# Four more pairs of FFN blocks in seven half-size products, with a load list of their own for the weight parts

## The chip, the core and the metric

The kernel runs on one core of one Trainium2 chip, as one program. The metric is device time in microseconds (us), median of three runs. TensorE (PE) multiplies, VectorE (DVE) and ScalarE (ACT) work on tiles, GpSimd (POOL) does small work and issues a few transfers, and SyncE (SP) issues nearly all of them. Each engine takes its instructions in the order of its own program and waits for semaphores of the others.

## The reference, cut to what matters

A two-layer decoder trunk on 256 tokens of width 1024, in float32, with four SwiGLU FFNs of hidden width 2816:

```python
def swiglu(h, w_gate, w_up, w_down):
    return (jax.nn.silu(h @ w_gate) * (h @ w_up)) @ w_down

for layer in range(2):
    x = x + 0.5 * swiglu(rms_norm(x, ffn1_norm[layer]), ...)
    h = rms_norm(x, mix_norm[layer])
    mem_n = rms_norm(mem, mem_norm[layer])
    x = x + (mlstm_mixer(h, mem_n, ...) if layer == 0 else dilated_mixer(h, mem_n, k_sh, v_sh, ...))
    x = x + 0.5 * swiglu(rms_norm(x, ffn2_norm[layer]), ...)
    if layer == 0:
        kv = rms_norm(x, kv_norm) @ w_kv      # shared keys (QK-normed) and values, used by layer 1
```

The dilated mixer adds a bias by distance to its scores; both mixers also attend to the 256 memory tokens.

## The kernel before, in words

**One product in three passes.** Operands are float32; each is split into a high part (a rounded copy, ScalarE) and a low part (the rest, VectorE), and a product is the sum of three passes, low by high, high by high and high by low (`mm3`, L773). Most passes are 128x512: 128 rows of the contraction, 512 columns of weights.

**Weight units.** Weights come in units of 128x1024 (512 KB) in the order in which PE uses them (`_stream`, L100). A unit is loaded by SP into one of six `raw` tiles, split by ScalarE (`hi`, 1024 columns) and VectorE (`lo`), and stands in a ring of eight `hi`/`lo` pairs until PE has used it (`emit_unit`, L631). So the two engines can be at most eight units ahead of PE.

**An FFN.** Its width is cut into eleven blocks of 256 (`FB`). `g b` multiplies both halves of the tokens (t = 0, 1) with gate and up of block b: four units, 2 x 8 x 3 = 48 products, into PSUM banks named `gups`. ScalarE makes the silu (`sil`), VectorE the hidden block `h`, which goes to DRAM and back turned (`hb`, `hd`, `ht`; `placed`, L1036), and is split (`hhb`, `hlb`). `d b` multiplies it with the down weights: two units, 24 products into `acc`. A plan orders the `g`, `d` and other steps (`_plan`, L81); the order of the instructions on each engine is then set by a planner in the kernel that carries its own estimate of each engine's clock (`_Model`, L241 on) and emits what is ready first.

**Pairs in seven products.** Two FFNs, named (layer, which) = (0,2) and (1,2), take blocks 5 and 6 together. The contraction is cut in two and the two blocks' weights and the two halves of x are combined so that seven products of half length stand for eight (a form of Strassen's method). Step `mb` of a plan is product m of the pair that begins with block b, so `25` is product 2 of the pair (5, 6). Each is 4 row chunks x 3 passes = 12 products on PE from two units, so a pair takes 84 in place of 96. What it needs beside:
- Sums and differences of x, once per FFN (`sums`, L1102; tiles `xs`, `xd`, `th`, `tl`).
- Three kinds of weight parts in two row groups (k = 0, 2): slot a (`pa`), b (`pb`) and c (`pc`), loaded by SP, some with a second part added on top by a transfer from POOL (`next_part`, L584), and remade by VectorE between the products (`remade`, L609): a-b after product 5, then b+a after 3, c-a after 4; b also takes another part by an adding transfer from POOL. `SLOTS` says which product uses which slot; every one of the fourteen units is split as usual.
- Combinations of the seven results (`seventh`, L1130): `e` is a copy of product 2, then `g` is product 5 plus `e`; products 4, 3 and 7 go on adding to the PSUM banks of 2, 5 and 1, so 4 waits for the copy, 3 for the first `g`, and 7 for the third `g`, the one that reads product 1. VectorE makes five more such sums (`c21`, `c12`, `f`, `c22`, `c11`), and four hidden blocks come out.

The order in which the products come is 2, 5, 4, 3, 1, 6, 7 in all plans.

**When parts are loaded.** Parts stand in the same list as the other units; one pair is open at a time (`self.open`), and while other units are loaded every third of them pulls one part from `todo` (`early`, L595, `EVERY = 3`), at most fourteen units early.

**The attention of layer 1.** After FFN (0,2), `shared_kv` (L1662) makes keys (`kTs`), values (`vs`) and the bias, which lies as a table of differences in DRAM (`diag`) and is read into a tile `bias`. All three stay in SBUF through FFN (1,1) until `mixer_b` (L1716). The eight chunks of mixer B's output weights are split in advance during (0,2) and (1,1), in steps called `pre` (`AHEAD_OF`), stored as `wo` in DRAM and reloaded in mixer B.

Of the kernel before, what the change touches and what calls it, by code (L numbers as in the profile page):

```python
# [48 lines left out]
AHEAD_OF = {(0, 2): (9,), (1, 1): (2, 3, 4, 5, 6, 7, 8)}  # L49

PLANS = {(1, 2): "g0 g1 g2 d0 g3 d1 g4 d2 25 55 45 35 d3 15 65 d4 75 g7 g8 d5 d6 g9 d7", (0, 2): "g0 g1 g2 d0 g3 d1 g4 25 55 d2 45 35 d3 15 65 d4 75 g7 g8 d5 d6 g9 d7"}
# [6 lines left out]
EVERY = 3  # L61
# [3 lines left out]

SLOTS = {2: ("a", (0,), None), 5: ("b", (3,), None), 4: ("c", (2, 0), None),
# [14 lines left out]
def _plan(layer, which):  # L81
# [4 lines left out]
    for what, b in ((s[0], int(s[1:])) for s in PLANS.get((layer, which), default).split()):  # L86
# [8 lines left out]
        if what == "d" and b + 2 in AHEAD_OF.get((layer, which), ()):  # L95
            plan.append(("pre",))
# [144 lines left out]
class _Model:  # L241
# [71 lines left out]
    def product(self, columns, cycles, rows, outs, ins):  # L313
# [9 lines left out]
        self.run("tensor", cycles / (2400 if self.fast else 1200) + 0.0027, outs, ins)  # L323

    def run(self, engine, cost, outs, ins, delay=0.0):
# [8 lines left out]
        for a in outs:  # L334
            self.mark(a, end, True, engine)
        self.latest = max(self.latest, end)


class _Engine:
# [5 lines left out]
    def __getattr__(self, method):  # L345
        call, model, name = getattr(self.engine, method), self.model, self.name

        def traced(out, *args, **kw):
# [8 lines left out]
            if name == "sync" or name == "gpsimd" and method == "dma_start":  # L357
                model.run("sync", max(n * out.partition_size() * 4 / 360e3, 0.06), outs, ins, 2.0)
# [51 lines left out]
class _Kernel:  # L410
    def __init__(self, tc, ctx, io, out, units):
# [18 lines left out]
        self.stored, self.slots, self.made, self.open, self.partp = {}, {}, {}, None, None  # L430
        self.todo, self.turn = [], 0
# [123 lines left out]
    def load_unit(self):  # L555
        i, self.loaded = self.loaded, self.loaded + 1
        if self.units[i][1] is None:
            return
        width = self.units[i][2]
        if self.units[i][1][0] == "parts":  # L560
            self.load_part(i)
            return
# [7 lines left out]
    def load_part(self, i):  # L570
        key = self.units[i][0]
        if self.open != key[1:4]:
            self.begin_parts(key[1:4])
        slot = SLOTS[key[4]][0], key[5]
        while slot not in self.slots:
            self.next_part()
        self.raw[i] = self.slots[slot]

    def begin_parts(self, pair):
        self.open = pair  # L580
        self.slots = {}
        self.todo = [(m, k) for m, k in ((4, 0), (2, 0), (4, 2), (2, 2), (5, 0), (5, 2))]

    def next_part(self):  # L584

        m, k = self.todo.pop(0)
        slot, parts, _ = SLOTS[m]
        t = self.work.tile([P, 1024], F32, tag="mem", name="pa") if slot == "a" else \
            self.partp[1].tile([P, 1024], F32, tag=f"p{slot}{k}", name=f"p{slot}{k}")
        self.slots[slot, k] = t  # L590
        self.nc.sync.dma_start(t, self.part_of(self.open + (parts[0], k)))
        for p in parts[1:]:
            self.nc.gpsimd.dma_start(t, self.part_of(self.open + (p, k)), accum_op=ALU.add)

    def early(self):  # L595

        for i in range(self.loaded, min(self.next + EARLIER, len(self.units))):
            key, src = self.units[i][:2]
            if src and src[0] == "parts" and self.open is None and self.may_load(i):
                self.begin_parts(key[1:4])  # L600
        self.turn += 1
        if self.todo and (self.todo[0][0] != 5 or self.summed) and self.turn % EVERY == 0:
            self.next_part()
# [5 lines left out]
    def remade(self, pair, m, k):  # L609

        nc = self.nc
        a, b, c = (self.slots.get((n, k)) for n in "abc")
# [9 lines left out]
        elif m == 7 and k == 2:  # L622
            self.open = None
# [7 lines left out]
    def emit_unit(self):  # L631
# [48 lines left out]
        while self.loaded <= i:  # L680
            self.room()
            self.load_unit()
        if src is None:
# [12 lines left out]
    def loads(self):  # L696

        while self.loaded < len(self.units) and self.loading() < RAW and \
                (self.units[self.loaded][1] is not None or self.loaded == self.next) and \
                self.may_load(self.loaded):  # L700
            self.load_unit()
            self.early()
# [4 lines left out]
    def may_load(self, i):  # L707

        key, src = self.units[i][:2]
        return src is None or src[0] != "parts" or \  # L710
            self.open in (None, key[1:4]) and self.partp is not None and \
            self.partp[0] == key[1:3] and (key[4] != 5 or self.summed)

    def room(self):
        while self.loading() >= RAW:
            self.finish(self.running[0])
        key, src = self.units[self.loaded][:2]
        if not self.may_load(self.loaded):
            self.finish(self.made[self.open, 7, 2])

    def unit_ready(self):
# [8 lines left out]
        if i not in self.raw:  # L730
            return 1e9
        key = self.units[i][0]
# [4 lines left out]
        at = max(model.ready(self.raw[i][:, :self.units[i][2]]),  # L737
# [248 lines left out]
    def ffn(self, layer, which, after, memory=None):  # L986
        with ExitStack() as ctx:
            self.partp = None
            self.ffn_in(layer, which, after, memory, self.pool(ctx, f"ffn{layer}{which}"))

    def ffn_in(self, layer, which, after, memory, fp):
# [6 lines left out]
        pairs = (layer, which) in PLANS  # L998

# [11 lines left out]
        def hidden(b, t):  # L1011
            def steps(ps):
# [6 lines left out]
                hh = self.work.tile([P, FB], F32R, tag="hh", bufs=5, name="hh")  # L1019
                hl = self.work.tile([P, FB], F32R, tag="hl", bufs=5, name="hl")  # L1020
# [15 lines left out]
        def placed(b, before):  # L1036
# [7 lines left out]
            yield  # L1044
            hh = fp.tile([P, 4, 4, 32], F32R, tag="hh", bufs=4, name="hhb")
# [22 lines left out]
        def dn(b, t):  # L1068
# [5 lines left out]
            parts = hT.pop((b, t))  # L1074
# [901 lines left out]
```

## Time and profile before

| | us |
|---|---|
| runs | 985.94, 984.80, 982.86 |
| median | 984.8 |
| span of the profiled execution | 981.7 |
| median less that span | 3.1 |

The span runs from the first to the last instruction of one profiled execution; the runs' times are of the whole execution. A matmul's time in the trace overlaps the next one's, since they are pipelined, so the cost of one is the distance between starts. In the rows, `out<-in` names tiles by the program's names, `xN` is a count, and what stands in square brackets or behind a bar is the engine's idle time before it and what ended that.

### The profile page before, as it was taken

The page shows a single profiled execution, that of the slowest core. Times are in us where ns is not written, and L with a number is a line of the kernel's source. Part 1 is how long each engine was busy: PE and PEld are TensorE (multiplying, and loading weights), DVE is VectorE, ACT ScalarE, POOL GpSimd, SP SyncE. Part 2 cuts the span into 40 slices and gives each one's busy share as a digit, 9 for nine tenths or more (in the row PEclk, how much of TensorE's full clock was granted, in tenths as well). Part 3 has the DMA queues.
Part 4 walks back from the last instruction along what each step waited for, and adds up shares of the span by engine and source line. Part 5 has one row for each costly group of instructions (what it writes and reads, how often), then busy time and mean ns, then how long its engine had stood idle before and what let it go on. Part 6 is the DMA issues. An engine that isn't in the chain of part 4 may idle for free.

```text
span 981.7 us, 13154 instructions
## 1 busy us (share of the span) xinstructions
PE 973.7 (99%) x4655; PEld 809.8 (82%) x4655; DVE 691.0 (70%) x1035; ACT 563.8 (57%) x903; POOL 52.2 (5%) x86
## 2 busy tenths in 40 slices
PE   9999999999999999999999999999999999999998
PEld 6888888899998888888878888888887788878887
DVE  5856656569886787976586677776576679589653
ACT  7656445477565655655466566565564585465541
POOL 0002000010010000000011000000002000000000
PEclk9999999999999999999999999999999999999999
DMA  9968677346355697388657688889627557945751
GB/s 353 321 212 302 212 239 227 112 148 230 118 193 193 202 318 243 116 290 268 235 179 252 226 318 274 336 301 316 246 86 266 207 175 252 375 99 205 272 166 43
DMA packets 85482, 223.95 MB, mean 228 GB/s; under 512 B 8172, under 2 KB 29608, under 8 KB 85416
## 3 DMA queue, kind: packets, MB, share of 16 engines
q1 hardware_dynamic: 84120, 218.88, 64.5%
q0 software_dynamic: 1152, 4.19, 2.3%
q8 instruction: 36, 0.59, 0.3%
q14 instruction: 30, 0.25, 0.1%
q10 hardware_dynamic: 144, 0.04, 0.0%
HBM read 203.66 MB, written 19.42 MB: 227 GB/s over the span
## 4 chain that ended last, share of the span: by engine, by line
PE 95%; DVE 2%; ACT 1%; DMA 1%; issue 1%; SPq 0%; DVEq 0%; ACTq 0%
PE gups L763 47%; PE acc L763 24%; PE aps L763 8%; PE oacc L763 4%; PE kvps L763 3%; PE bqps L763 2%; PE mkvps L763 2%; PE tps L770 1%; DVE s L349 1%; PE po L763 1%; PE tpp L770 1%; PE sc L763 1%; DMA ht<-hd 0%; PE ms L763 0%; PE pn L763 0%
## 5 line engine op out<-in xcount | busy, mean ns | idle before, releaser
L349 DVE TENSOR_TENSOR lo<-raw,hi 128x1024 fp32r<-128x1024 f32 (+2 forms) x263 | 302.7, 1167 | 85.2 <-ACT hi L349 79.7
L349 ACT CAST hi<-raw 128x1024 fp32r<-128x1024 f32 (+2 forms) x263 | 260.1, 1008 | 95.3 <-PE acc L763 40.9
L763 PE MATMUL gups<-lo,xh 128*128 128x512 f32 x656 | 254.9, 391 | 1.6 <-DVE g L349 1.6
L763 PE MATMUL gups<-hi,xh 128*128 128x512 f32 x656 | 254.6, 390 | 0.4 <-ACT hi L349 0.4
L763 PE MATMUL gups<-hi,xl 128*128 128x512 f32 x656 | 254.4, 390 | 0.0
L763 PEld LDWEIGHTS gups<-lo,xh 128*128 128x128 f32 x656 | 123.2, 188 | 27.3 <-DVE g L349 2.1
L763 PEld LDWEIGHTS gups<-hi,xh 128*128 128x128 f32 x656 | 123.3, 188 | 26.4 <-ACT hi L349 1.3
L763 PEld LDWEIGHTS gups<-hi,xl 128*128 128x128 f32 x656 | 123.4, 188 | 26.0
L349 ACT ACTIVATE sil<-gups,rstd 128x256 f32<-128x256 f32 x84 | 39.7, 474 | 146.4 <-PE gups L763 136.3
L763 PE MATMUL acc<-lo,hhb 128*128 128x512 f32 x304 | 119.5, 393 | 0.0
L763 PE MATMUL acc<-hi,hlb 128*128 128x512 f32 x304 | 118.6, 390 | 0.1
L763 PE MATMUL acc<-hi,hhb 128*128 128x512 f32 x304 | 118.3, 389 | 0.0
L349 DVE SCALAR_TENSOR_TENSOR lo<-raw,gains,hi 128x512 fp32r<-128x512 f32 x144 | 99.6, 744 | 16.4 <-ACT hi L349 16.1
L349 DVE SCALAR_TENSOR_TENSOR h<-gups,rstd,sil 128x256 f32<-128x256 f32 x84 | 40.0, 480 | 91.1 <-ACT sil L349 91.0
L349 ACT ACTIVATE hi<-raw,gains 128x512 fp32r<-128x512 f32 x144 | 93.9, 715 | 14.9 <-PE gups L763 5.8
L763 PEld LDWEIGHTS acc<-hi,hlb 128*128 128x128 f32 x304 | 57.1, 188 | 12.4 <-DVE hlb L349 0.5
L763 PEld LDWEIGHTS acc<-lo,hhb 128*128 128x128 f32 x304 | 57.1, 188 | 11.6 <-ACT hhb L349 0.3
L763 PEld LDWEIGHTS acc<-hi,hhb 128*128 128x128 f32 x304 | 57.1, 188 | 11.4
L763 PE MATMUL aps<-lo,xh 128*128 128x384 f32 (+1 forms) x144 | 49.8, 346 | 0.0
L763 PE MATMUL aps<-hi,xl 128*128 128x384 f32 (+1 forms) x144 | 47.5, 330 | 0.0
L763 PE MATMUL aps<-hi,xh 128*128 128x384 f32 (+1 forms) x144 | 47.4, 329 | 0.0
L349 ACT CAST hhb<-ht 128x512 fp32r<-128x512 f32 x38 | 23.5, 619 | 26.4 <-DMA ht<-hd 26.3
(228 smaller groups left out, 1191.2 us busy)
## 6 DMA issues: line engine op xcount, KB each, us to landing
raw<-in_wts SPq DMA_DIRECT2D x294, 512.0 KB, 5.1
raw<-in_wts SPq DMA_DIRECT2D x32, 384.0 KB, 3.8
hd<-hb SPq DMA_DIRECT2D x38, 256.0 KB, 5.6
ht<-hd SPq DMA_DIRECT2D x38, 256.0 KB, 4.6
wo<-hi SPq DMA_DIRECT2D x8, 512.0 KB, 6.7
wo<-lo SPq DMA_DIRECT2D x8, 512.0 KB, 7.3
hi<-wo SPq DMA_DIRECT2D x8, 512.0 KB, 5.5
lo<-wo SPq DMA_DIRECT2D x8, 512.0 KB, 7.2
```

Source lines behind the costliest of these rows:

```text
L349: call(out, *args, **kw)
L763: self.pe.matmul(out, lhsT=lhsT, rhs=rhs, start=start, stop=stop, skip_group_check=more)
L770: self.pe.transpose(out, in_, ident)
```

## The change

Pairs are taken in all four FFNs: one (blocks 5, 6) in (0,1) and (1,1), two (5, 6 and 7, 8) in (0,2) and (1,2); that is six in place of two. The plan of (1,1) is the one that (1,2) had. In (0,2) and (1,2) products 2 and 5 of the first pair are now followed by three down blocks.

```diff
-PLANS = {(1, 2): "g0 g1 g2 d0 g3 d1 g4 d2 25 55 45 35 d3 15 65 d4 75 g7 g8 d5 d6 g9 d7", (0, 2): "g0 g1 g2 d0 g3 d1 g4 25 55 d2 45 35 d3 15 65 d4 75 g7 g8 d5 d6 g9 d7"}
+PLANS = {
+    (0, 1): "g0 g1 g2 g4 p d0 g3 25 55 d1 d2 45 d4 35 "
+            "d3 p 15 p 65 75 g7 p g8 d6 g9 p d5 d7",
+    (0, 2): "g0 g1 g2 g3 25 55 d0 d1 d2 45 35 15 65 75 "
+            "d3 g9 g4 27 57 d5 47 37 17 67 77 d4 d9 d6",
...
+LEAD = 3.0
+SOON = 8
+TWICE = ((0, 1), (0, 2), (1, 2))
+SUMS = {(0, 1): 30.0, (0, 2): 16.0, (1, 1): 8.0, (1, 2): 8.0}
```

`p` in a plan is a `pre` step; there are five, all in (0,1), in place of eight in (0,2) and (1,1). So five of mixer B's eight output chunks are reloaded from DRAM, and three are loaded and split there.

The weight parts leave the list of the other units. All parts of an FFN's pairs stand in one list, and the next is loaded when its slot's last user is done and when it is needed within eight units or SP's clock, by the planner's estimate, is less than 3 us ahead. Slot a has two sets of tiles in turn where `TWICE` says so.

```diff
+    def part_ready(self):
+
+        if not self.todo:
+            return False
+        p, m, k = self.todo[0]
+        if self.index[("st",) + self.pairs[p] + (2, 0)] > self.next + EARLIER:
+            return False
+        if SLOTS[m][0] == "b" and not self.summed:
+            return False
+        chains = [self.made.get(c) for c in self.before_part()]
+        if not all(c is not None and c.done for c in chains):
+            return False
+        return self.index[("st",) + self.pairs[p] + (m, k)] <= self.next + SOON or \
+            self.model.clock["sync"] < self.now + LEAD
...
             self.load_unit()
-            self.early()
+        while self.part_ready():
+            self.next_part()
```

Two costs in the planner change: a warm three-pass product gets a gap of 13.3 ns in place of 2.7, and an adding transfer is reckoned twice as long and 3 us to land.

Keys and values go to DRAM when they are made, and these and the bias are read into mixer B's own tiles when it opens:

```diff
+        def kept(chains):
+            yield from self.wait(*chains)
+            for a in (kT, v):
+                self.kept.append(self.dram.tile([P, 2 * MW], F32, name="kept"))
+                nc.sync.dma_start(self.kept[-1], a.rearrange("p a b -> p (a b)"))
...
     def mixer_b(self, after):
...
+            for a, kept in zip((self.kT, self.v), self.kept):
+                nc.sync.dma_start(a.rearrange("p a b -> p (a b)"), kept)
+            nc.sync.dma_start(self.bias, bass.AP(self.diag.tensor, self.diag.offset,
+                                                 [[1, P], [384, 12], [1, 256]]))
```

The split hidden blocks of both kinds share four buffers in the FFN's own memory (before: five tiles in a common pool for the kind of (0,1)'s first blocks), with a limit so that no more than four wait for their down block:

```diff
+        def room(*key):
+
+            while len(pending) >= 4:
+                yield 0.05
+            pending.add(key)
```

Small tiles of both mixers that used those five take their own. In all, PE's program has 4,476 matmul instructions, transposes counted, in place of 4,524, VectorE's 1,135 instructions in place of 1,037 and ScalarE's 878 in place of 846; POOL issues 24 adding transfers in place of 8.

More of the change, by code (lines that the diff above doesn't have):

```diff
@@ L85, in _plan @@
     plan, left = [], list(range(NB - 1))
-    for what, b in ((s[0], int(s[1:])) for s in PLANS.get((layer, which), default).split()):
+    for what, b in ((s[0], int(s[1:] or 0)) for s in PLANS.get((layer, which), default).split()):
+        if what == "p":
+            plan.append(("pre",))
+            continue
         if what in "1234567":
@@ L335, in run, with adding @@
             self.mark(a, end, True, engine)
+        self.latest = max(self.latest, end)
+    def adding(self, cost, outs, ins):
+        start = max([self.clock["sync"]] + [self.ready(a, True, "sync") for a in outs])
+        self.clock["sync"] += cost
+        end = start + cost + 3.0
+        for a in outs:
+            self.mark(a, end, True, "sync")
         self.latest = max(self.latest, end)
@@ L357, in traced @@
             if name == "sync" or name == "gpsimd" and method == "dma_start":
-                model.run("sync", max(n * out.partition_size() * 4 / 360e3, 0.06), outs, ins, 2.0)
+                cost = max(n * out.partition_size() * 4 / 360e3, 0.06)
+                if kw.get("accum_op") is None:
+                    model.run("sync", cost, outs, ins, 2.0)
+                else:
+                    model.adding(2 * cost, outs, ins)
                 return
@@ L568, in load_unit, with begin_parts @@
         self.raw[i] = raw
[L570 to L582, printed above, removed]
+    def begin_parts(self, layer, which, plan, pool):
+        self.partp, self.slots = pool, {}
+        self.twice = (layer, which) in TWICE
+        self.pairs = [(layer, which, s[1]) for s in plan if s[0] == "st" and s[2] == 2]
+        self.todo = [(p, m, k) for p in range(len(self.pairs)) for m, k in PARTS]
@@ L584, in next_part @@
     def next_part(self):
-        m, k = self.todo.pop(0)
+        p, m, k = self.todo.pop(0)
         slot, parts, _ = SLOTS[m]
[L588 to L603, printed above, removed]
+        if slot == "a" and (not self.twice or p % 2 == (self.pairs[p][:2] == (0, 1))):
+            t = self.work.tile([P, 1024], F32, tag="mem", name="pa")
+        else:
+            t = self.partp.tile([P, 1024], F32, tag=f"p{slot}{k}", name=f"p{slot}{k}")
@@ L605, in part_of @@
+        pair = self.pairs[p]
+        self.slots[pair, slot, k] = t
+        self.nc.sync.dma_start(t, self.part_of(pair + (parts[0], k)))
+        for i in parts[1:]:
+            self.nc.gpsimd.dma_start(t, self.part_of(pair + (i, k)), accum_op=ALU.add)
     def part_of(self, part):
@@ L682, in emit_unit @@
             self.load_unit()
+        if src is not None and src[0] == "parts":
+            slot = key[1:4], SLOTS[key[4]][0], key[5]
+            while slot not in self.slots:
+                self.finish(*[self.made[c] for c in self.before_part()])
+                self.next_part()
+            self.raw[i] = self.slots[slot]
         if src is None:
@@ L1074, in dn @@
             parts = hT.pop((b, t))
+            if t == 1 or not turned(layer, which, b):
+                pending.remove((b, t))
             last = b == NB - 1
             groups = [(slice(h * 512, (h + 1) * 512), acc[t][h], b == 0, last) for h in range(2)]
-            if (layer, which, t) == (1, 2, 1) and b >= NB - 2:
+            if (layer, which, t) == (1, 2, 1) and b in (left[1], NB - 1):
                 f, a, begins, _ = groups.pop()
```

96 lines of the change are left out of this document (47 added, 49 removed), and 4 rows, old and new, of the table PLANS.

## The prediction

> **What bounds the kernel now.** The page first: who is busy, and what the chain that ended last is made of.
>
> ```profile
> span 981.7 us, 13154 instructions
> PE 973.7 (99%) x4655; PEld 809.8 (82%) x4655; DVE 691.0 (70%) x1035; ACT 563.8 (57%) x903; POOL 52.2 (5%) x86
> PEclk9999999999999999999999999999999999999999
> PE 95%; DVE 2%; ACT 1%; DMA 1%; issue 1%; SPq 0%; DVEq 0%; ACTq 0%
> ```
>
> The product engine is 95% of that chain, at full clock in every slice. A busy PE alone would not prove that it is saturated, so next the chain in order of time (start, us, what) and PE's own waits (total, times, longest).
>
> ```profile
> 45.77 10.88 PE gups L763 x48
> 56.66 5.44 PE acc L763 x24
> ...
> PE gups L763 <- DVE g L349: 1.6, 1, 1.6
> ...
> PE po L763 <- ACT mp L349: 0.7, 1, 0.7
> ```
>
> 48 products of 128x512 take 10.88 us, 226.7 ns each, end to end, and the longest wait of PE in the list is 1.6 us. So a product removed is worth 226.7 ns, and a microsecond lost elsewhere counts only if PE runs out of work. It does so for longer than 0.7 us at one place, inside the pair of the last FFN (start, us):
>
> ```profile
> 877.54 0.39 PE L763 MATMUL gups<-hi,xl 128*128 128x512 f32 x1
> 879.56 0.50 PE L763 MATMUL gups<-lo,xh 128*128 128x512 f32 x1 [1.64 <-DVE g L349]
> 879.90 0.39 PE L763 MATMUL gups<-hi,xh 128*128 128x512 f32 x1
> ...
> 877.68 1.23 DVE L349 TENSOR_TENSOR pb<-pb,pa 128x1024 f32<-128x1024 f32 x1
> 878.82 0.68 DVE L349 TENSOR_TENSOR g<-gups,e 128x512 f32<-128x512 f32 x1
> ...
> 869.02 0.62 ACT L349 CAST hhb<-ht 128x512 fp32r<-128x512 f32 x1 [4.18 <-DMA ht<-hd]
> ```
>
> Two starts 2.02 us apart, so 1.8 us lost. Product 3 waited for `g`, which stood on VectorE behind the remakes of the parts, and VectorE was late since ScalarE, which works in order, had stood 4.18 us for a transfer. The other pair lost nothing, though VectorE was busy 40.12 of 44 us there (columns: length, then busy us of PE, PEld, DVE, ACT, POOL, clock, DMA share, GB/s):
>
> ```profile
> 375.00:419.00 44.00, 44.00 (x196) 36.44 (x195) 40.12 (x45) 26.01 (x31) 1.73 (x2) 1.00 0.49 145
> 848.00:883.00 35.00, 33.36 (x148) 27.30 (x147) 26.42 (x30) 19.59 (x23) 1.72 (x2) 1.00 0.59 170
> ```
>
> **The products removed.** Two ordinary blocks are 96 products (2 halves of x, 8 row chunks, 3 passes each); seven half-size ones are 7x12 = 84. Four more pairs: 4x12 = 48 fewer, and PE's two programs differ by 48 matmul instructions (4,524 and 4,476). 48 x 226.7 ns = **-10.9 us**. PE has no cover for them, so this is certain.
>
> **What a pair costs VectorE.** Rows by shape (busy us, mean ns):
>
> ```profile
> L349 DVE TENSOR_TENSOR lo<-raw,hi 128x1024 fp32r<-128x1024 f32 x220 | 265.0, 1219 | 76.8 <-ACT hi L349 71.5
> L349 DVE TENSOR_TENSOR pa<-pa,pb 128x1024 f32<-128x1024 f32 x4 | 4.9, 1218 | 0.0
> L349 DVE TENSOR_TENSOR g<-gups,g 128x512 f32<-128x512 f32 x6 | 4.1, 676 | 0.0
> L349 DVE SCALAR_TENSOR_TENSOR h<-gups,rstd,sil 128x256 f32<-128x256 f32 x84 | 40.0, 480 | 91.1 <-ACT sil L349 91.0
> L349 DVE STREAM_TRANSPOSE hb<-h 128x256 f32<-128x256 f32 x76 | 33.4, 441 | 7.2 <-DMA hd<-hb 6.2
> L349 DVE TENSOR_TENSOR hlb<-ht,hhb 128x512 fp32r<-128x512 f32 x38 | 26.0, 684 | 14.2 <-ACT hhb L349 14.1
> ```
>
> A pair: 14 splits x 1.22, 6 remakes x 1.22, 6 sums from PSUM x 0.68, 4 x (0.48 + 0.44) = 32.2 us, against 84 x 0.2267 = 19.0 us of PE: short by 13.2. What stands between its products gives back: a down block 5.44 - (2 x 1.22 + 0.68) = 2.3 us; an ordinary block 10.88 - (4 x 1.22 + 2 x 0.92) = 4.2. The rest has to have been split ahead into the ring of 8, 8 x 1.22 = 9.8 us at most. Counting down blocks between 2 and 7: before, FFN (0,2) has three, short by 6.3, no wait; (1,2) has two, short by 8.6, 1.8 us. After: (0,1) has four, 4.0 short; (0,2) and (1,2) each have a first pair with three (6.3) and a second with one (10.9); (1,1) has two (8.6). The first pairs and (0,1) are like the one that lost nothing. The second pairs begin behind an ordinary block, g4, whose four splits serve 10.88 us, so their ring holds more PE time; they are the worst two all the same.
>
> Which add is waited for also moves. On VectorE in the last FFN, `lo` is a split, `pa pb pc` the parts, `gups` the PSUM banks; first before, around the add to which product 3 is bound:
>
> ```order
> L349 TENSOR_TENSOR pc0_7901<-pc0_7901,pa_7985 128x1024
> L349 TENSOR_TENSOR lo327_8334<-pb0_8082,hi327_8333 128x1024
> L349 TENSOR_TENSOR pb0_8082<-pb0_8082,pa_7985 128x1024
> L349 TENSOR_TENSOR pc2_8043<-pc2_8043,pa_8069 128x1024
> L349 TENSOR_TENSOR lo328_8363<-pb2_8084,hi328_8362 128x1024
> L349 TENSOR_TENSOR pb2_8084<-pb2_8084,pa_8069 128x1024
> L349 TENSOR_TENSOR g_8373<-gups_8347,e_8345 128x512
> ```
>
> And after, the first pair of the same FFN:
>
> ```order
> L369 TENSOR_TENSOR lo333_8281<-raw333_8047,hi333_8280 128x1024
> L369 TENSOR_TENSOR lo334_8287<-raw334_8060,hi334_8286 128x1024
> L369 TENSOR_TENSOR g_8307<-gups_8273,e_8271 128x512
> L369 TENSOR_TENSOR lo335_8318<-raw335_8074,hi335_8317 128x1024
> L369 TENSOR_TENSOR lo336_8321<-pc0_8178,hi336_8320 128x1024
> L369 TENSOR_TENSOR pc0_8178<-pc0_8178,pa_7828 128x1024
> ```
>
> `g` has left its place behind the remakes and has three down blocks of cover, so the wait of 1.8 us goes: **-1.8**. Late next is the add from product 1 to product 7. In the pair of the last FFN, before, it is the `g` from `gups` and `g`:
>
> ```order
> L349 TENSOR_TENSOR lo336_8476<-raw336_8147,hi336_8475 128x1024
> L349 STREAM_TRANSPOSE hb_8487<-h_8436 128x2x4x32
> L349 STREAM_TRANSPOSE hb_8489<-h_8465 128x2x4x32
> L349 TENSOR_TENSOR g_8373<-gups_8461,g_8373 128x512
> L349 TENSOR_TENSOR lo337_8479<-pc0_7901,hi337_8478 128x1024
> ```
>
> And after, in its second pair:
>
> ```order
> L369 TENSOR_TENSOR hlb_8899<-ht_8884,hhb_8898 128x4x4x32
> L369 TENSOR_TENSOR lo368_8905<-pb0_8432,hi368_8904 128x1024
> L369 TENSOR_TENSOR e_8832<-gups_8805,g_8851 128x512
> L369 TENSOR_TENSOR lo369_8912<-pb2_8445,hi369_8911 128x1024
> L369 SCALAR_TENSOR_TENSOR h_8926<-gups_8805,rstd_7811,sil_8927 128x256
> L369 TENSOR_TENSOR g_8851<-gups_8834,g_8851 128x512
> L369 TENSOR_TENSOR lo370_8933<-pc0_8457,hi370_8932 128x1024
> L369 STREAM_TRANSPOSE hb_8948<-h_8926 128x2x4x32
> L369 TENSOR_TENSOR lo371_8937<-pc2_8489,hi371_8936 128x1024
> L369 SCALAR_TENSOR_TENSOR h_8950<-gups_8834,rstd_7634,sil_8951 128x256
> L369 TENSOR_TENSOR g_8851<-gups_8940,g_8851 128x512
> ```
>
> Between 1 and 7 stood 6, d4 (8.2 us of PE); now only 6 (2.72 us), in five of six pairs, and in the second pairs an `hlb` that waits for a transfer stands shortly ahead. No row shows that wait; its bounds are 0 (375 to 419) and per pair 1.8 (877), in the second pairs 1.8 + (10.9 - 8.6) = 4.1. I take 1.8 for each second pair and 0.9 for (1,1), between its two likenesses since the columns of its `g` stand earlier: **+4.5**, bounds 0 and 6 x 1.8 = 10.8.
>
> **Transfers.** Rows: KB, us to landing, and queues (packets, MB, share).
>
> ```profile
> hd<-hb SPq DMA_DIRECT2D x38, 256.0 KB, 5.6
> ht<-hd SPq DMA_DIRECT2D x38, 256.0 KB, 4.6
> ...
> pb<-in_wts SPq DMA_DIRECT2D x4, 512.0 KB, 6.4
> pb<-in_wts POOLq DMA_DIRECT2D x4, 512.0 KB, 7.1
> bias<-diag SPq DMA_DIRECT2D x1, 1536.0 KB, 8.4
> ...
> q1 hardware_dynamic: 84120, 218.88, 64.5%
> q0 software_dynamic: 1152, 4.19, 2.3%
> ```
>
> The 16 more adding transfers from POOL are 8.4 MB at 2.3/4.19 = 0.55% per MB, 4.6%; eight loads fewer on SP and six tiles of `wo` that are neither stored nor reloaded give back 10.5 MB at 0.29%, 3.1%; the 16 engines are not full. POOL's queue is in order and stands before a part that has not landed; behind it in (1,1) are the norms of the memory's keys, first used in mixer B, elsewhere `rstd` at the end of the FFN, tens of us later. The first blocks of (0,1) now stand in another order, at the same bytes per us of products. The moved tiles and the limit of four blocks that are split ahead make nobody wait who has the down blocks' 5.44 us in hand. All of it zero, with that cover; without it a late part holds PE for the 7.1 us of its landing. A POOL transfer landed 0.7 us later than SP's (7.1 and 6.4), in stages with VectorE at up to 91%; 0.7 us ahead of a use that is a product or more off (2.72 us) adds nothing. The Trainium skill ("SBUF — State Buffer", SBUF: two separate sides) speaks against more DMAs from POOL: VectorE can lock GpSimd out while it writes their descriptors, for the whole of an instruction. [...]
>
> Keys, values and bias: stored once, reloaded when mixer B opens. On SP, in mixer B, after:
>
> ```order
> L369 DMA raw301_6940<-in_wts 128x1024
> L369 DMA kTs_7051<-kept_5333 128x1536
> L369 DMA vs_7052<-kept_5335 128x1536
> L369 DMA bias_7053<-diag_5115 128x12x256
> L369 DMA hi302_7174<-wo0_696 128x1024
> ```
>
> Before, only the bias was loaded, once, as soon as it was made. Now the three wait at mixer B's opening for the FFN's memory, and behind them on SP stand the weights of the output projection. At that opening the transfers stood still, and the first user of the bias came later (rows: opening, first query products, first user; and the rate at the kernel's start):
>
> ```profile
> 720.00:735.00 15.00, 15.00 (x74) 12.45 (x73) 11.70 (x19) 12.28 (x24) 1.87 (x4) 1.00 0.02 6
> ...
> 727.75 2.77 PE bqps L763 x12
> ...
> 744.49 1.64 DVE L349 SCALAR_TENSOR_TENSOR s<-pa,rqb,bias 128x128 f32<-128x128 f32 x6 [2.74 <-PE pa L763]
> ...
> 763.57 1.27 DVE L349 SCALAR_TENSOR_TENSOR s<-pa,rqb,bias 128x256 f32<-128x256 f32 x3 [2.48 <-PE pa L763]
> ...
> 5.00:46.00 41.00, 40.59 (x179) 33.35 (x179) 32.48 (x51) 31.76 (x58) 1.74 (x4) 1.00 0.97 355
> ```
>
> The three are 0.79 + 0.79 + 1.57 = 3.15 MB; at 355 GB/s 8.9 us, one after another by the rows 2 x 6.4 + 8.4 = 21 us. From 727.75 that is 737 to 749, against 744.5. I take zero, being nearer the first (nothing else moves), and up to 4 for the range. Only five of eight output chunks are now split in advance, so three splits fall into mixer B: two before `s`, in the 2.48 us in which VectorE waits anyway, one between `s` and its maximum, where it delays: **+1.1**, bounds 0 and 3 x 1.22 = 3.7.
>
> **Sum.** The profiled execution's span is 981.7 us; the median of the runs, 984.8 (982.9 to 985.9), lies 3.1 above it, which I take for what lies around the span. -10.9 - 1.8 + 4.5 + 1.1 = -7.1: a span of 974.6 and a time of **977.7 us**. About 0.3%, 2.95 us, can be told from no change by measuring this kernel.
>
> **Rivals.** (1) *The ring covers all pairs.* Then -12.7: 972.1. For it stands 40.12 of 44 without a wait; against it, the second pairs. (2) *ScalarE stands for `ht` in every pair*, as at 869.02, and each pays 1.8: -12.7 + 10.8 + 1.1 = -0.8, **984.0**, no change. Against: it happened to one pair of two. (3) *VectorE becomes the bound, slower.* If the ring holds only 4 tiles' worth of lead (4.9 us) when a pair begins, each waits for its shortage less 4.9: 0, 1.4, 6.0, 3.7, 1.4, 6.0, together 18.5: -12.7 + 18.5 + 1.1 = +6.9, **991.7**. It decides from a lead under some 5.6 us, where the waits exceed 15. For it: VectorE's shortages add to 47 us; against it: 848 to 883, where two down blocks and a stalled ScalarE cost 1.8, not 3.7. (4) *The clock falls.* The opening row has nine matmuls of 512 columns in 4.02 us, about 0.43 us each:
>
> ```profile
> 1.25 4.02 PE L1867 MATMUL warm<-warm 128*128 128x512 bf16 x9 [1.25 <-DVE warm L349]
> ```
>
> After the gap of 2.02 us, PE went on at 0.23 us. If both second pairs wait 4.2 us and then run as long at 0.43 us, losing 2.0 more, the sum is -12.7 + 2 x 6.2 + 4 x 0.9 + 1.1 = +4.4, 989.2. The Trainium skill ("TensorE: Matmul & The Clock Gate", What's actually happening) has the clock fall to half after an idle window of about 3.4 us; by it the gap of 2.02 us had to leave the clock alone, which the row shows, and a 4.2 us wait would not. That the change does not remove what it says is excluded by the order.
>
> **How the numbers follow.** Forecast 0.60, with its own ends 974 and 981.5 (new waits between 0.8 and 8.3 us); (1) 0.18; (2) 0.13; (3) 0.06; (4) 0.03. Faster by over that bound: forecast and (1), 0.78; the same: (2), 0.13; slower: (3) and (4), 0.09. The range 971.5 to 984.5 holds the forecast, (1) and most of (2), and takes in 4 us for a late bias.
>
> **What would show it.** 48 products fewer at 226.7 ns; no wait on `g` for product 3 in (0,2) and (1,2); PE's waits, if any, ahead of product 7 or of the down block behind it in the second pairs, ended by VectorE; ScalarE standing for `ht` shortly before; bias landed before `s`. Wrong would be a PE gap over 4 us, gaps ended by a load, or a pitch other than 226.7 ns.

## The result, and the profile after

The changed kernel takes **1006.9 us** (median of four runs, 1005.8 to 1008.8); the kernel before, on the same chip, 983.8 (982.8 to 985.9). The ratio is 1.0236, 95% interval 1.0216 to 1.0256: 23 us slower, where 977.7 was forecast. The span of the profiled execution is 1003.9 us, 22.2 more than before.

The page of the changed kernel, in the lines that answer to those shown of before, with the group of the split of a turned block on ScalarE and, last, the way of a turned block through DRAM:

```profile
span 1003.9 us, 13192 instructions
PE 974.9 (97%) x4607; PEld 804.8 (80%) x4607; DVE 773.3 (77%) x1133; ACT 591.1 (59%) x935; POOL 72.1 (7%) x102
PEclk9999999999999999989999999999999999999999
PE 61%; DMA 16%; DVE 13%; issue 5%; ACT 4%; POOL 1%; SPq 1%; DVEq 0%; ACTq 0%; POOLq 0%
L369 ACT CAST hhb<-ht 128x512 fp32r<-128x512 f32 x38 | 23.6, 621 | 69.2 <-DMA ht<-hd 69.2
hd<-hb SPq DMA_DIRECT2D x38, 256.0 KB, 5.4
ht<-hd SPq DMA_DIRECT2D x38, 256.0 KB, 4.2
```

48 matmuls are gone, but PE's share of the chain that ended last fell from 95% to 61%, and DMA and VectorE have taken 29%. By their medians the two turning transfers land as fast as before (5.6 and 4.6 then), yet ScalarE stood 69.2 us for them, against 26.3. The slowest of them took longer; both kinds together, before and after:

```profile
DMA to landing us min/median/max: 2.0/5.3/8.5
...
DMA to landing us min/median/max: 2.0/5.0/13.3
```

ScalarE also stood 55.1 us for weights (`raw` 27.7, `pb` 19.6, `pc` 7.8), against 6.8. Of PE's own waits (total, times, longest) the longest had been 1.6 us; now:

```profile
PE gups L787 <- DVE h L369: 12.2, 5, 4.6
PE tpk L794 <- DVE kn L369: 5.0, 3, 2.9
PE acc L787 <- ACT hhb L369: 2.2, 2, 1.8
...
PE gups L787 <- DVE g L369: 0.3, 1, 0.3
```

PE waits for `h`, which frees a PSUM bank, and for `kn`, the memory's keys, which it transposes (`tpk`). The five waits on `h` stand where a pair begins, ahead of its product 2 or 5: in (0,2) 1.24 us in the first pair and 4.62 in the second, in (1,2) 3.20 in the first and 0.67 and 2.50 in the second. The wait on `g` before product 3 has gone, as forecast; ahead of product 7 there is one, of 0.3 us, at 401 us in the first pair of (0,2).

**Where the time went, by stage.** A stage runs from its first product's start to the next stage's; the first begins and the last ends with the span. "Saved" is 2.7 us (12 products) for each added pair.

| stage | before | after | saved | lost |
|---|---|---|---|---|
| FFN (0,1) | 199.9 | 200.0 | 2.7 | 2.8 |
| mixer A | 119.5 | 121.4 | | 1.9 |
| FFN (0,2) | 179.8 | 190.7 | 2.7 | 13.6 |
| keys and values | 35.6 | 36.2 | | 0.6 |
| FFN (1,1) | 192.7 | 194.0 | 2.7 | 4.0 |
| mixer B | 70.8 | 73.1 | | 2.3 |
| FFN (1,2) | 183.4 | 188.5 | 2.7 | 7.8 |

In (1,2) the 1.8 us of the old wait on `g` went too, so 9.6 came in its place. In all 33.0 us were lost and 10.8 saved. The FFNs hold 28.2 of the loss, and the two with two pairs 21.4.

**The longest wait.** It lies in (0,2) where the second pair begins. The chain that ended last, in that stretch (start, us, what):

```profile
410.96 9.58 DMA hd<-hb
...
422.99 2.32 DVE lo L369 x2
...
426.36 1.22 DVE lo L369
427.58 1.13 DVE pa L369
428.72 0.60 DVE hlb L369
429.32 0.03 DVE h L369
429.35 4.94 DMA ht<-hd
434.29 0.02 issue
434.31 0.63 ACT hhb L369
...
436.01 2.26 DVE lo L369 x2
438.27 0.41 DVE h L369
...
438.72 3.36 PE gups L787 x7
```

Read it downwards. Block 5 is 9.58 us on its way out to DRAM, behind six weight loads that SP issued just before, while VectorE stands 4.9 us (0.56 and 1.35 for splits whose loads are late, 3.02 for the buffer that this transfer frees). From 420.64 VectorE works without a break through splits and remakes until it reaches `hlb`, the low part of block 5, 2.2 us after ScalarE's high part. Only then is the one `ht` tile free, and SP can fetch block 6 (4.94 us). ScalarE's next instruction is the split of block 6, and it stands for that; VectorE's next is the low part of it, and it stands too. When both go on, VectorE must catch up with two splits before it reaches `h`, for which PE has been waiting. In the engines' own rows the standing reads:

```profile
434.31 0.62 ACT L369 CAST hhb<-ht 128x512 fp32r<-128x512 f32 x1 [7.54 <-DMA ht<-hd]
...
434.96 0.69 DVE L369 TENSOR_TENSOR hlb<-ht,hhb 128x512 fp32r<-128x512 f32 x1 [5.25 <-ACT hhb L369]
```

So the chain holds two things that take turns: transfers stop VectorE, and VectorE's load delays the next transfer. Block 6 isn't needed by its down block until much later; only the order on ScalarE and VectorE makes it urgent.

The waits at 926 and 932 us have the same shape (ScalarE stood 6.88 us for `ht`). The 3.20 us in the first pair of (1,2) do not: there ScalarE and VectorE stood for a weight part, and two remakes and four splits came before `h`:

```profile
857.20 1.05 ACT L369 CAST hi<-pb 128x1024 fp32r<-128x1024 f32 x1 [2.34 <-DMA pb<-in_wts]
...
858.28 1.23 DVE L369 TENSOR_TENSOR lo<-pb,hi 128x1024 fp32r<-128x1024 f32 x1 [2.43 <-ACT hi L369]
```

By the chain, SP issued that load only when it had sent off a hidden block, and that block had stood behind an `hlb`.

**The clock.** Three waits of PE and what followed, by starts:

```profile
438.72 0.80 PE L787 MATMUL gups<-lo,th 128*128 128x512 f32 x1 [4.62 <-DVE h L369]
439.31 0.63 PE L787 MATMUL gups<-hi,th 128*128 128x512 f32 x1
439.74 0.63 PE L787 MATMUL gups<-hi,tl 128*128 128x512 f32 x1
...
865.64 0.50 PE L787 MATMUL gups<-lo,th 128*128 128x512 f32 x1 [3.20 <-DVE h L369]
865.97 0.40 PE L787 MATMUL gups<-hi,th 128*128 128x512 f32 x1
866.21 0.40 PE L787 MATMUL gups<-hi,tl 128*128 128x512 f32 x1
...
931.97 0.73 PE L787 MATMUL gups<-lo,th 128*128 128x512 f32 x1 [2.50 <-DVE h L369]
932.50 0.63 PE L787 MATMUL gups<-hi,th 128*128 128x512 f32 x1
932.93 0.63 PE L787 MATMUL gups<-hi,tl 128*128 128x512 f32 x1
```

After the waits of 4.62 and 2.50 us the starts are 0.43 us apart, after 3.20 they are 0.24. Behind the opening, 26 products started 0.41 to 0.43 us apart, in four places, each behind one of PE's waits (the shortest 1.85 us); at 0.2 us more each that is about 5 us of the loss.

### The profile page after: what moved, and what is told of

The parts are those of the page before. It is cut to its first block, busy times and chain, and to the rows that moved or that the text cites. A ratio compares the mean times of both kernels' runs of the same rounds, so it can differ in the third digit from the quotient of the medians.

```text
span 1003.9 us, 13192 instructions
## 1 busy us (share of the span) xinstructions
PE 974.9 (97%) x4607; PEld 804.8 (80%) x4607; DVE 773.3 (77%) x1133; ACT 591.1 (59%) x935; POOL 72.1 (7%) x102
## 4 chain that ended last, share of the span: by engine, by line
PE 61%; DMA 16%; DVE 13%; issue 5%; ACT 4%; POOL 1%; SPq 1%; DVEq 0%; ACTq 0%; POOLq 0%
PE gups L787 25%; PE acc L787 17%; PE aps L787 6%; DVE lo L369 6%; DMA ht<-hd 5%; DMA hd<-hb 5%; PE oacc L787 4%; PE kvps L787 3%; DMA pb<-in_wts 2%; DMA raw<-in_wts 2%; ACT hi L369 2%; PE bqps L787 2%; PE tps L794 1%; DVE h L369 1%; DVE hb L369 1%
## 5 line engine op out<-in xcount | busy, mean ns | idle before, releaser
L369 DVE TENSOR_TENSOR lo<-raw,hi 128x1024 fp32r<-128x1024 f32 (+2 forms) x239 | 271.9, 1159 | 58.6 <-ACT hi L369 56.9
L369 ACT CAST hi<-raw 128x1024 fp32r<-128x1024 f32 (+2 forms) x239 | 233.0, 1003 | 66.6 <-DMA raw<-in_wts 26.2
L787 PE MATMUL gups<-lo,xh 128*128 128x512 f32 x552 | 214.2, 391 | 0.0
L787 PE MATMUL gups<-hi,xh 128*128 128x512 f32 x552 | 214.1, 390 | 0.0
L787 PE MATMUL gups<-hi,xl 128*128 128x512 f32 x552 | 214.0, 390 | 0.0
L787 PEld LDWEIGHTS gups<-hi,xh 128*128 128x128 f32 x552 | 103.8, 188 | 22.1 <-ACT hi L369 0.8
L787 PEld LDWEIGHTS gups<-hi,xl 128*128 128x128 f32 x552 | 103.9, 188 | 21.7
L787 PEld LDWEIGHTS gups<-lo,xh 128*128 128x128 f32 x552 | 104.0, 188 | 21.4
L787 PE MATMUL acc<-hi,hlb 128*128 128x512 f32 x304 | 119.3, 393 | 0.0
L369 ACT ACTIVATE sil<-gups,rstd 128x256 f32<-128x256 f32 x76 | 35.9, 472 | 69.2 <-PE gups L787 56.0
L787 PEld LDWEIGHTS acc<-lo,hhb 128*128 128x128 f32 x304 | 57.5, 189 | 15.5 <-ACT hhb L369 3.1
L787 PE MATMUL gups<-lo,th 128*128 128x512 f32 x128 | 52.9, 413 | 12.5 <-DVE h L369 12.2
L369 ACT CAST hhb<-ht 128x512 fp32r<-128x512 f32 x38 | 23.6, 621 | 69.2 <-DMA ht<-hd 69.2
L369 ACT CAST hi<-pb 128x1024 fp32r<-128x1024 f32 x36 | 37.4, 1050 | 26.9 <-DMA pb<-in_wts 19.6
L787 PE MATMUL gups<-hi,th 128*128 128x512 f32 x128 | 51.8, 405 | 0.0
```

The source lines that it names most:

```text
L369: call(out, *args, **kw)
L787: self.pe.matmul(out, lhsT=lhsT, rhs=rhs, start=start, stop=stop, skip_group_check=more)
```

## The experiments

Theory 1: the turned blocks come late, ScalarE and VectorE stand for them in their order, and PE pays. Theory 2, the rival: VectorE's load in the pairs. Theory 3: the new code (load list, keys and values through DRAM, the limit on split blocks) costs by itself. Theories 4 (the order that the planner makes with its new gap) and 5 (full transfer queues, so that weights come late) were added after the first runs. All ratios are to the kernel before, run beside them.

### Pairs taken out again

Two pairs, with the plans of before and all the new code (the five `pre` steps stay in (0,1)):

```diff
+    (0, 2): "g0 g1 g2 d0 g3 d1 g4 25 55 d2 45 35 d3 15 65 d4 75 g7 g8 d5 d6 g9 d7",
+    (1, 2): "g0 g1 g2 d0 g3 d1 g4 d2 25 55 45 35 d3 15 65 d4 75 g7 g8 d5 d6 g9 d7",
-    (0, 1), (1, 1): ...
```

> The new load list, keys and values through DRAM, five output chunks in (0,1) stay; the plans are those of before, with the two old pairs (48 products, 10.9 us, more than the changed kernel). Theory 1 (the hidden blocks' way through DRAM is late in the stages with pairs and ScalarE and VectorE, which work in order, stand for it): few such stages are left, so within 5 us of before, 979 to 989. Theory 2 (VectorE's load in the pairs): the same, 981 to 987. Theory 3 (the new list or the reloads cost by themselves, wherever the pairs stand): 995 or more.

Four pairs: (0,2) and (1,2) have those two plans, the other two FFNs keep the change's:

> The second pairs of (0,2) and (1,2) are taken out, and these two FFNs have their plans of before: four pairs in place of six, 24 products (5.4 us) more than the changed kernel. Theories 1 and 2 alike put most of the 31.7 us that PE lost in gaps and at half clock into the second pairs: 1007 + 5 - 22 = 990, range 984 to 995. Theory 3 (each pair costs alike through its transfers and its list): a third of the loss goes, 1007 + 5 - 11 = 1001.

Measured: 998.9 (1.0150, 1.0131 to 1.0168) and 990.7 (1.0078, 1.0038 to 1.0119). The second agrees with theories 1 and 2, though its five runs lie as far apart as 985.7 and 998.7. The first does not, and has the number of theory 3: with the old pairs alone the new code was 15 us slower than before, and in the FFN (1,1), which has no pair there, 4.9 us were lost. So something besides the pairs costs, and ScalarE's standing had even grown. The group of `hhb` in the run with two pairs:

```profile
L364 ACT CAST hhb<-ht 128x512 fp32r<-128x512 f32 x38 | 23.6, 621 | 109.7 <-DMA ht<-hd 109.6
```

### Two direct tries at theory 1

The planner reckons a later landing, so that it places the splits later; and a second `ht` tile:

```diff
-                    model.run("sync", cost, outs, ins, 2.0)
+                    turning = out.tensor.name.startswith(("hd", "ht"))
+                    model.run("sync", cost, outs, ins, 5.0 if turning else 2.0)
```

> One number of the planner: the turning transfers of the hidden blocks are reckoned to land 5.0 us after their cost and not 2.0, so that the splits of a turned block are put later in ScalarE's and VectorE's order. All six pairs stay, and VectorE's work. Theory 1: ScalarE's 69 us of standing for the turned block fall below 40, and PE's long gaps with them: 985 to 997. Theory 2: the same load on VectorE, so within 4 us of 1007.

```diff
-            ht = fp.tile([P, 4, P], F32, tag="ht", bufs=1, name="ht")
+            ht = fp.tile([P, 4, P], F32, tag="ht", bufs=2, name="ht")
```

> The turned block's tile gets a second buffer, so that the second block of a pair is fetched without waiting until the first one is split. Theory 1: the second of a pair's blocks comes some 5 us earlier, and the gaps at 433, 861 and 928 us shrink: 990 to 1000. Theory 2: within 4 us of 1007.

Measured: 1017.0 (1.0345, 1.0318 to 1.0372) and 998.3 (1.0145, 1.0128 to 1.0162). The second tile brought 8.6 us, as theory 1 has it, and cut the standing to 52.6 us. The later landing did what it should to ScalarE, 23.7 us of standing instead of 69.2, and the time rose by 10: now PE waited for the split blocks themselves. From its list of waits:

```profile
PE acc L788 <- ACT hhb L369: 14.0, 6, 5.2
PE gups L788 <- DVE lo L369: 4.3, 2, 2.8
```

My expectation was wrong there, and with it the use of ScalarE's standing as a measure of the loss.

### The planner's gap

What was left of the change in the run with two pairs was mostly the planner. With 13.3 ns it reckons 512/2400 + 0.0133 = 0.2267 us for a warm product, which is the measured distance of starts; with 2.7 ns it reckons 0.216. First the kernel before, with that one number of the change:

```diff
-        self.run("tensor", cycles / (2400 if self.fast else 1200) + 0.0027, outs, ins)
+        gap = 0.0133 if self.fast and ins[0].dtype == F32R else 0.0027
+        self.run("tensor", cycles / (2400 if self.fast else 1200) + gap, outs, ins)
```

> The kernel before, with one number of the change: the planner reckons 13.3 ns between warm products in place of 2.7. Nothing else moves but the order that the planner makes of it. Theory 4 (new, from the run with two old pairs, in which ScalarE stood 110 us for turned blocks against 26: with a slower PE in its estimate the planner puts the splits of the turned blocks ahead of ScalarE's work that follows PE, so ScalarE meets the transfers unlanded): 990 to 998, and ScalarE standing 80 us or more for `ht`. Theory 3 (the load list, keys and values through DRAM, the limit on split blocks): 981 to 987 and 26 us.

The reverse, in the run with two pairs, and 5 ns in the changed kernel:

```diff
-        gap = 0.0133 if self.fast and ins[0].dtype == F32R else 0.0027
+        gap = 0.0027
```

> The run with the two old pairs (998.9), with the planner's old 2.7 ns. The new load list, keys and values through DRAM and five output chunks in (0,1) stay. Theory 4: 984 to 989, with 2 to 4 us of it left in mixer B, which had the gaps of 1.2 and 1.3 us. Theory 3: within 4 us of 999.

> The changed kernel, all six pairs, with 5 ns in place of 13.3 in the planner. Theory 4: 990 to 998, with ScalarE's 69 us of standing for `ht` halved. Theory 2 (VectorE's load in the pairs): within 4 us of 1007.

Measured: 992.9 (1.0093, 1.0070 to 1.0117); 984.3 (1.0004, 0.9993 to 1.0014); 1006.0 (1.0225, 1.0202 to 1.0248). The number alone costs the kernel before 9.5 us, and taking it back frees the run with two pairs of its whole loss, 14.6 us. Theory 3 is out: the load list, the reloads and the limits cost nothing in sum when the pairs are the old two. But in the changed kernel the number does nothing that can be told, 1006.0 against 1006.9.

By stage, what belongs to the number is clear in mixer A: 121.4 to 121.8 us in the runs with 13.3 ns so far, 119.3 to 119.6 with 2.7 or 5. In the kernel before with the new gap the 8.4 us of span lie in (0,1), 3.4, mixer A, 2.3, mixer B, 1.9, and little in the FFNs with pairs. ScalarE's standing rose to 63.0 us, but not in proportion: in (0,1) it rose from 2.8 to 15.5, and the stage lost 3.4; in (0,2) from 3.8 to 21.1, and the stage lost 0.7. With one pair there, standing is nearly free. Theory 4 is right that the order costs; its mechanism is possible for (0,1), is contradicted in (0,2), and isn't shown. In the changed kernel 5 ns moved time and did not save it: mixer A and the keys are 2.7 us shorter, (0,1) and (1,2) 5.6 longer.

### VectorE's load

```diff
         elif m == 3:
-            nc.vector.tensor_tensor(b, b, a, ALU.add)
+            pass
         elif m == 4:
             yield from self.wait(self.made[pair, 5, k])
-            nc.vector.tensor_tensor(c, c, a, ALU.subtract)
+            pass
```

> The changed kernel without the parts' second and third remakes (b+a after product 3, c-a after product 4): 24 instructions of VectorE, 29 us, go, and the products 6 and 7 multiply parts that are not the right ones. Theory 2: half or more of the 31.7 us that PE lost goes, 985 to 992. Theories 1 and 4 (late transfers, order): 1000 to 1008.

Measured: 1001.8 (1.0187, 1.0159 to 1.0214). 27 us of VectorE's busy time went (773.3 to 746.4) and the kernel got 5.1 us faster. Alone, this part of VectorE's load isn't it.

### Other ways for the transfers

Blocks 5 and 6 of (0,2) and (1,2) turned by TensorE; `ht` issued by GpSimd; `hd` by ScalarE (both with two `ht` tiles); four `raw` tiles:

```diff
+    if which == 2 and b in (5, 6):
+        return False
     return b < NB - 1 and ((layer, which) != (0, 1) or b > 1)
...
```

> The changed kernel, in which blocks 5 and 6 of (0,2) and (1,2) are turned by TensorE's transposes and not through DRAM; these are the turned blocks that ScalarE stands for when the second pair begins. It adds 16 transposes, about 3 us with their splits. Theory 1 (the way through DRAM is late): the long gaps at 433 and 862 us go, 990 to 998. A theory 5 (the transfer queues are full in the stages with pairs, and the loads of weights are what is late): the gaps stay and are ended by loads or their splits, 1003 to 1012.

```diff
-            nc.sync.dma_start(ht, bass.AP(d.tensor, d.offset, [[P, P], [32 * 512, 4], [1, P]]))
+            nc.gpsimd.dma_start(ht, bass.AP(d.tensor, d.offset, [[P, P], [32 * 512, 4], [1, P]]))
```

> The run with two tiles for the turned block (998.3), with the second of the two turning transfers (`ht`) issued by GpSimd, so that SP never stands for `hd` to land and the weight loads behind it go at once. If SP's standing is what makes the stages late: 985 to 993. If it is only the transfers' own time, or GpSimd's in-order queue with the added parts holds `ht` back: 998 or more.

```diff
-            nc.sync.dma_start(d, hb.rearrange("p j c t e -> p (j c t e)"))
+            nc.scalar.dma_start(d, hb.rearrange("p j c t e -> p (j c t e)"))
```

> The run with two tiles for the turned block (998.3), with the first of the two turning transfers (`hd`) issued by ScalarE, so that it doesn't queue behind up to six weight loads of SP. If this backlog makes the turning late (theory 1, in the form that the trace shows at 403 to 416 us): 985 to 994, and ScalarE's standing for `ht` under 35 us. If ScalarE's own standing for `hb` costs as much: 998 or more.

```diff
-RAW = 6
+RAW = 4
```

> The changed kernel with four tiles for weight units on their way in place of six, so at most four loads stand ahead of a turning transfer. Theory 1: `hd` lands 2 us or more sooner, 995 to 1004. Theory 5: the loads are late already, and with fewer of them in flight the time rises to 1010 or more.

Measured: 1004.2 (1.0221, 1.0182 to 1.0260), 1016.1 (1.0317, 1.0273 to 1.0360), 1012.2 (1.0280, 1.0249 to 1.0312) and 1026.8 (1.0440, 1.0406 to 1.0473). All four went against theory 1's numbers. With TensorE turning the blocks the gap at 433 us did vanish, and (0,2) got 3.3 us shorter, but (1,2) got 2.0 longer, and the wait at 862 stayed (3.6 us): I had laid it to the wrong blocks, since it stands in the first pair. `hd` from ScalarE landed in 5.7 us, no sooner than the 5.4 from SP, and ScalarE stood for `hb` besides. So another queue does not help as a whole. Whether SP's standing costs anywhere is not shown: against the run with two tiles, the two runs lose most in (1,1) (8.0 and 10.4 us), where PE waits up to 5.8 us for the memory's keys (`tpk`), and with `hd` from ScalarE (1,2) is 2.0 us shorter. The times with TensorE turning and with four tiles lie where theory 5 had put them. With four tiles, so with at most four weight loads ahead of it, `hd` landed no sooner either (5.8 us by the median). That run shows what fewer loads in flight cost; ScalarE's wait for weights in it (27.7 us in the changed kernel):

```profile
ACT hi L369 <- DMA raw<-in_wts: 98.0, 76, 11.2
```

### Not waiting at all, and both causes at once

Here the splits read a tile of x that is there anyway; the transfers still run, unread. And, apart from it, the adding transfers left out (both places that issue them):

```diff
-                                  ht.rearrange("p i (c e) -> p i c e", c=4))
+                                  self.x[0][:, 0:512].rearrange("p (i c e) -> p i c e", i=4, c=4))
```

> The changed kernel, whose turned blocks still go to DRAM and back, but the splits `hhb` and `hlb` read a tile of x that is there anyway and not the turned block, so no engine waits for it; the output is not the reference's. Theory 1 (standing for the turned blocks): 975 to 988. Theory 5 (the transfers' load makes everything late): 997 to 1007, with PE's waits ended by parts or raw units.

```diff
-        for i in parts[1:]:
+        for i in ():
...
-            nc.gpsimd.dma_start(b, self.part_of(pair + (1, k)), accum_op=ALU.add)
+            pass
```

> The changed kernel without the 24 adding transfers from GpSimd (12.6 MB); parts b and c lack their second and third terms, so the output is not the reference's. Theory 5: 985 to 997, and `hd` and `ht` land 1 us sooner. Theory 1: within 5 us of 1007.

Measured: 994.1 (1.0098, 1.0070 to 1.0127) and 1003.7 (1.0199, 1.0178 to 1.0220). Theory 5 falls as the main cause: 12.6 MB fewer gain 3.2 us where it expected 10 to 22, and the unread kernel moves every byte. That full queues make single transfers late remains possible. Theory 1 gets 12.8 us, more than any other single edit of the six pairs, but about half of what it expected (the middle of 975 to 988). Then this edit together with the left-out remakes:

> The changed kernel, in which the splits of the turned blocks read a tile of x and so don't wait, and VectorE's second and third remakes (24 instructions, 29 us) are left out; the output is not the reference's. If the two causes add: 994 - 5 = 989, 986 to 992. If VectorE's load is what is left once nobody stands for the turned blocks: 974 to 983. If the rest is order and queues: 990 to 995.

Measured: **980.2** (0.9973, 0.9961 to 0.9985). The two edits gained 12.8 and 5.1 us alone and 26.7 together, 8.8 more than their sum. So both causes count, and each hides the other's cure. The stretch from 360 to 480 us, which is mostly FFN (0,2) with its two pairs, first of the changed kernel, then without the remakes, then unread, then both (columns as in the prediction):

```profile
360.00:480.00 120.00, 113.19 (x485) 92.13 (x484) 102.94 (x119) 67.87 (x81) 7.11 (x8) 0.97 0.72 227
```

```profile
360.00:480.00 120.00, 111.61 (x480) 90.93 (x479) 93.51 (x111) 67.41 (x80) 7.09 (x8) 0.97 0.75 236
```

```profile
360.00:480.00 120.00, 117.05 (x510) 94.95 (x508) 104.87 (x121) 69.09 (x83) 7.10 (x8) 1.00 0.76 245
```

```profile
360.00:480.00 120.00, 118.19 (x520) 96.84 (x519) 95.41 (x111) 70.71 (x83) 7.10 (x8) 1.00 0.78 249
```

Without the remakes VectorE has 9.4 us more room and PE does no more matmuls (480 against 485), since the engines still stand for the turned blocks. Unread, the standing for turned blocks is gone and PE does 510; with both, 520. The whole stage (0,2) took 190.7, 187.7, 184.1 and 178.9 us in the four. ScalarE still stands 39.7 us for weights in the last kernel, and it takes 980.2 all the same. In it the four FFNs together take 748.1 us; the changed kernel took 773.2, and full cover, from before, would be 755.8 - 10.9 - 1.8 = 743.1. One reserve holds: both edits also change the order that the planner makes, since it reckons the unread splits as ready at once, and an order alone was worth 9.5 us in the kernel before.

### Fewer pairs, for a kernel faster than both

Three pairs: the two old ones and one in (1,1), old gap, two `ht` tiles; the same with two pairs; four pairs with 5 ns and two `ht` tiles. The edits are those above.

> The planner's old 2.7 ns, the two old pairs with their plans of before, one pair in (1,1) (whose plan is the one that (1,2) had) and two tiles for the turned block. 12 products fewer than before, 2.7 us. If each pair by itself is covered as long as the order is that of the old gap: 979 to 983. If a pair costs more in waits than it saves in any FFN: 985 to 990.

> The run with two old pairs and the old gap (984.3), with two tiles for the turned block. If the single tile makes ScalarE wait in ordinary blocks too: 981 to 983. If only blocks of a pair come two at a time: 984 to 985.

> Four pairs (one in each FFN, (0,2) and (1,2) with their plans of before), 5 ns in place of 13.3 in the planner, two tiles for the turned block. 24 products fewer than before, 5.4 us. If the second pairs and the planner's gap are the two things that lose: 977 to 982. If a pair in (0,1) and (1,1) costs what it saves in any order: 983 to 990.

Measured: 984.8 (1.0010, 0.9999 to 1.0022), 984.9 (1.0015, 1.0005 to 1.0025), 985.0 (1.0013, 1.0003 to 1.0023). None beats the kernel before. With four pairs the FFNs come to 753.9 us, 1.9 under before, where 5.4 of products went and 1.8 of the wait on `g`; mixer B takes 1.7 of that back. The second `ht` tile does nothing where the pairs are two (984.3 without it).

## Why the prediction was wrong, point by point

**The products removed, -10.9: right.** 48 fewer, and the starts of the others are still 227 ns apart where PE has work at full clock.

**The wait on `g`, -1.8: right.** The wait ahead of product 3 is gone; the one wait on `g` that is left is 0.3 us. The run with two pairs and the old gap has (1,2) at 181.9 us against 183.4.

**The new waits in the pairs, +4.5 with bounds 0 and 10.8: this step failed.** What the FFNs lost measures 30.0: 2.8 in (0,1), 13.6 in (0,2), 4.0 in (1,1), 9.6 in (1,2), among them the half-speed products. The 23.2 of (0,2) and (1,2) belong to this step; most of the 6.8 in the other two to the next. I counted VectorE's shortage against a ring that I took to be full, and looked for the late step among the adds (`g` before product 7). There 0.3 us came. What came late, 12.2 us in five waits, was `h` of the ordinary block ahead of a pair: in the second pairs behind an `hlb` that stood for a transfer, in the first pairs behind splits that stood for a weight part. I named that `hlb` ("shortly ahead") and left its price within the 1.8 us of the one case that the trace of before had. The upper bound did not even follow from my own figures: with 4.1 for each second pair it is 4 x 1.8 + 2 x 4.1 = 15.4, not 10.8. Nor was the one case a bound: VectorE was busy 26.42 of 35 us in it, and could catch up. In the 40 us that end 24 us before the longest wait of the changed kernel it had no room, and in the 10 us behind them it had room and stood for transfers:

```profile
370.00:410.00 40.00, 39.05 (x171) 31.64 (x170) 38.78 (x42) 23.55 (x28) 5.13 (x6) 1.00 0.93 277
```

**The transfers, zero with the down blocks' cover: right for the adding ones, wrong in who waits.** Without the adding ones 3.2 us are gained, and the turning ones land as before by their medians; single ones were slower (9.58 us ahead of the longest wait), but the run with two pairs and the old gap has one of 12.6 and loses nothing. The one `ht` tile, as before the change, makes the second block of a pair wait until VectorE has split the first, and I had priced that at nothing. The zero for (0,1) and (1,1) fell too: the norm of the memory's keys is waited for by PE's own transposes in the FFN (`tpk`, 5.0 us), not first in mixer B. In (0,1) VectorE stood there for GpSimd, whose first power of the norm (`rp_r`) shows 5.97 us; why isn't known. In (1,1) it was late since ScalarE and then VectorE stood. The rows of GpSimd, PE and ScalarE:

```profile
627.90 0.62 ACT L369 CAST hhb<-ht 128x512 fp32r<-128x512 f32 x1 [5.12 <-DMA ht<-hd]
...
628.80 0.47 ACT L369 ACTIVATE sq<-mkvps,memr 128x256 f32<-128x256 f32 x1
```

```profile
630.81 1.09 POOL L369 TENSOR_SCALAR rp_e<-hss 128x4 f32<-128x4 f32 x1 [2.65 <-DVE hss L369]
631.98 1.90 POOL L369 TENSOR_TENSOR rp_r<-rp_e,mhalf 128x4 f32<-128x4 f32 x1
```

```profile
635.64 0.69 PE L794 MATMUL tpk<-consts,kn 128*128 128x128 f32 x2 [2.86 <-DVE kn L369]
```

The square that the norm needs was done 5 us late on ScalarE, and no part transfer of GpSimd stood in between.

**Mixer B, +1.1: 2.3.** Within its bounds. With the two old pairs and the old gap it is 2.2, so it belongs to the new code there and not to the pairs.

**The planner's gap: no step at all.** I had it in the diff and gave it no price. It moves the order everywhere, and alone costs 9.5 us. In the changed kernel 2.5 us in mixer A and the keys can be laid to it; -10.9 - 1.8 + 30.0 + 2.3 + 2.5 = +22.1, and the span grew by 22.2 (a sum of stages, which must come out).

**The rivals.** Number 2 had the mechanism (ScalarE stands for `ht`) at 1.8 us a pair, 0.13; number 3 had VectorE as the bound, 0.06; number 4 the clock, 0.03. Something of all three happened, together, and I had reckoned each as if the others left it room to recover. Number 4's own figures (a wait of over 4 us, then 0.43) are in the rows, in one second pair of two. The mark that I set against myself, a gap over 4 us, was met; that VectorE would end PE's waits and that ScalarE would stand for `ht` shortly before was right.

**What stays open.** How much of the loss in the pairs is VectorE's load and how much late transfers can't be parted, since each edit also moves the order. The way from the gap's number to 9.5 us was not followed through. The 5.0 us still lost in the FFNs with both causes removed, and why three and four pairs give back what they save, are argued from stages only.

## What to carry to other kernels

When work is moved off a saturated engine, ask whether the engines that feed it can catch up after a stall, not only whether they have time on average: a stall that was free becomes a wait when its neighbour has lost its slack. If one ablation gains little, take two suspects away at once before acquitting either. A constant in a scheduler's cost model is a change like any other, and deserves a run by itself; here the number that fits the measured 227 ns made the old kernel slower.

## What the runs showed of the hardware

Behind a wait of 2.50 us the products started 0.43 us apart, and behind one of 3.20 us they did not. The granted clock (third number from the end) in three such stretches of the changed kernel, behind the waits of 4.62, 3.20 and 2.50 us:

```profile
437.00:444.00 7.00, 5.28 (x13) 4.14 (x14) 6.90 (x9) 6.02 (x8) 0.00 (x0) 0.51 0.74 225
866.00:872.00 6.00, 6.00 (x28) 4.94 (x27) 6.00 (x8) 3.15 (x4) 0.00 (x0) 1.00 1.03 251
932.00:935.50 3.50, 3.50 (x9) 2.73 (x10) 3.47 (x4) 2.19 (x3) 0.00 (x0) 0.51 0.30 122
```

The Trainium skill ("TensorE: Matmul & The Clock Gate", What's actually happening) has the clock fall after an idle window of about 3.4 us that runs freely. The first row, after 4.62 us, agrees. That 2.50 us were enough does not agree with a window that must be idle throughout; that 3.20 us were not enough agrees with windows at fixed places. So in this kernel the length of a wait alone doesn't tell whether the clock falls.
